# Hand-ordered engine queues, joint key products, token-major second phase and preloaded accumulation banks in a one-core diffusion layer

## The chip, the core and the metric

The kernel runs on one core of a Trainium2 chip. The metric is the device time of one execution in microseconds (us); the median of the runs shown is 2377.83 us. The engines are named as the profile names them: PE is TensorE, PEld its weight load, DVE VectorE, ACT ScalarE, POOL GpSimd, SP the engine whose queue issues the large loads.

## What is computed

One layer of a hybrid backbone over 256 latent tokens and 256 context tokens of width 4096, in float32:

```
mod  = silu(c) @ w_ada + b_ada           # shift, scale, gate: 3 x 4096, for latent and for context
h    = rmsnorm(x) * (1 + scale) + shift  # both streams
z    = h @ w_in                          # 13312 columns
A    = pointwise(silu(layernorm(depthwise31(val * sigmoid(glu)))))
B    = two RG-LRU scans (context first, its last state starts the latent scan)
C    = softmax(q k^T * s + bias) v       # 8x16 window of the latents and all 256 context keys
out  = rmsnorm(x + gate * (concat(A, B, C each * silu(gate path)) @ w_out))
```

From the context only the inputs of the scans (1024 columns), the keys and the values (2048 columns each) are needed. `w_ada` (4096 x 12288) is read once and multiplied by two vectors.

## The kernel before

Every large product takes its float32 operands as two float32r parts, high and low, and makes three passes (high times high, high times low, low times high), `gemm_cm` (L343) and `gemm_tm` (L360). The contraction of 4096 is cut into 32 tiles of 128. Weights come in loads of up to 4 tiles (1 MB, three buffers); ACT copies two tiles to the high part (L338), DVE subtracts to get the low part (L339).

- **Phase 1** goes over ten blocks of the contraction (`BLOCKS`), because the modulation of a tile must be known before its `h` can be made. In each block it makes ten chunks of 512 output columns: `r` (scan inputs, both streams, channel-major, 256-column products for each stream), `k` (keys, context alone, channel-major, 256 columns) and `v` (values, both streams, token-major, 512 columns). At the end of a chunk in a block its PSUM banks are added to SBUF pages by DVE (`spill`, L499; the first block's copies are ACT's, L497). Five banks, tag `g`, serve the chunks in turn.
- **Modulation** (`ada_units`) runs beside it: one load, then one unit of PE work. The two vectors are the stationary operand, padded to 32 columns; the moving operand is up to 512 columns of `w_ada`. Product `k` goes to column group `k % 4` of the array (L217), so that four products of a unit stand on the four groups. The tail of a unit sequence is a copy (L170), transposes (L175) and a sum. The second block of each pair after the eighth has its shift summed on DVE instead.
- **Phase 2** makes latent keys, queries, gates, conv inputs over the whole contraction, all channel-major with 256-column products, and between them the scans, the attention heads (L593 to L617), the depthwise convolution on DVE (L673) and its layer norm.
- **Phase 3** is the output projection, token-major with 512 columns, and the final norm.

The order on each engine is made by the tile framework's scheduler from the order of the code and from `high_priority` sections; `background` (L52) lets the loads of the modulation in at a set rate, `aside` (L490) puts a scan or a convolution between two chunks.

Of the kernel before, what the change touches and what calls it, by code (L numbers as in the profile page):

```python
# [10 lines left out]
F32 = mybir.dt.float32  # L11
# [17 lines left out]
PAIRED = 8  # L29
# [5 lines left out]
HP = 200000  # L35
# rates of the loads that go beside the products, by phase
ADA_A, ADA_B, CAP = 2.15, 1.2, 4.0
G1, G2, G3 = 0.4, 0.3, 0.4
# chunks of the last block that a recurrence follows; order of the second phase
REC1 = (1, 2, 4, 6, 8)  # L40
ORDER = "c0 c1 a0 a1 a2 n a3".split()
# [3 lines left out]
def tile_hybrid_layer(ctx: ExitStack, tc: tile.TileContext, x, c, cctx_tok, c_ctx, w_ada, b_ada,  # L45
# [9 lines left out]
    off = [0]  # L55
    hp = lambda: tc.high_priority(offset=off[0])
    bg = {"q": [], "rate": lambda w: 0.0, "credit": 0.0}

    def background(weight):
        """emits queued units of loads between those of the products, at the set rate"""  # L60
        bg["credit"] = min(bg["credit"] + bg["rate"](weight), CAP)
        while bg["q"] and bg["credit"] >= 2.0:
            bg["credit"] -= 2.0
            bg["q"].pop(0)()
# [5 lines left out]
    def bank(tag, name):  # L70
        uid[0] += 1
        return pp.tile([P, 512], F32, name=f"{name}_{uid[0]}", tag=tag, bufs=5 if tag == "g" else 3)

    def small(n, name):
        uid[0] += 1
        return sp.tile([P, n], F32, name=f"{name}_{uid[0]}", tag="small", bufs=8)

    wada = w_ada[0].rearrange("(k p) n -> p k n", p=P)
# [3 lines left out]
    V, A, S, G = nc.vector, nc.scalar, nc.sync, nc.gpsimd  # L82

    ident = cp.tile([P, P], F32, name="ident")
    make_identity(nc, ident)
    cols = cp.tile([P, 5, P], F32, name="cols")
    where = {}
    q128 = lambda v: v.rearrange("(r q) -> r q", q=P)
    cw_rows = conv_w[0].rearrange("k (t q) -> (k t) q", q=P)
    groups = [  # L90
        [("c", q128(c[0])), ("c_ctx", q128(c_ctx)), ("norm_g", q128(norm_g[0]))],
        [("b_ada", q128(b_ada[0])), ("ln_g", q128(ln_g[0])), ("b_pw", q128(b_pw[0])),
         ("rcb", rconv_b[0].rearrange("d (t q) -> (d t) q", q=P))],
        [("cw0", cw_rows[0:128])],
        [("cw1", cw_rows[128:248]), ("conv_b", q128(conv_b[0]))],
        [("ln_b", q128(ln_b[0])), ("rcw", rconv_w[0].rearrange("d j (t q) -> (d j t) q", q=P)),
         ("lam", lam[0].rearrange("d (t q) -> (d t) q", q=P)),
         ("b_i", b_i[0].rearrange("d (t q) -> (d t) q", q=P)),
         ("b_r", b_r[0].rearrange("d (t q) -> (d t) q", q=P))],
    ]  # L100

    def load_group(gi):
        t = page([P, P], name="rows")
        r = 0
        for name, ap in groups[gi]:
            n = ap.shape[0]
            A.dma_start(t[r:r + n], ap)
            where[name] = (gi, r)
            r += n
        ps = bank("aux", "psc")  # L110
        nc.tensor.transpose(ps[:, :r], t[:r], ident[:r, :r])
        V.tensor_copy(cols[:, gi, :r], ps[:, :r])

    def col(name, i, n=1):
        gi, r = where[name]
        return cols[:, gi, r + i:r + i + n]

    load_group(0)
    load_group(1)
    warm = cp.tile([P, 1], F32, name="warm")  # L120
    A.activation(warm, ident[:, 0:1], AF.Exp)

    # silu(c), silu(c_ctx) as channel columns, padded to 32 stationary columns
    scol = cp.tile([P, 64], F32, name="scol")
    cc64 = cols[:, 0, 0:64]
    V.tensor_scalar(scol, cc64, -80.0, None, ALU.max)
    A.activation(scol, scol, AF.Exp, scale=-1.0)
    V.tensor_scalar(scol, scol, 1.0, None, ALU.add)
    V.reciprocal(scol, scol)
    V.tensor_mul(scol, scol, cc64)  # L130
    cpad = [page([P, 16, 32], name="cpad") for _ in range(2)]
    for i in range(2):
        G.memset(cpad[i], 0.0)
        for s in range(2):
            V.tensor_copy(cpad[i][:, :, s:s + 1],
                          scol[:, 32 * s + 16 * i:32 * s + 16 * i + 16].rearrange("p (k o) -> p k o", o=1))
    sel = cp.tile([P, 2], F32, name="sel")
    for s in range(2):
        V.reduce_sum(sel[:, s:s + 1], ident[:, s:P:32], axis=AX.X)
    mask = cp.tile([P, 2, 64], F32, name="mask")  # L140
    A.dma_start(mask, masks)
    ones = cp.tile([P, 1], F32, name="ones")
    G.memset(ones, 1.0)
    tiny = cp.tile([P, 1], F32, name="tiny")
    G.memset(tiny, 1e-30)
    modG = cp.tile([P, KT, 2], F32, name="modG")
    modS = cp.tile([P, KT, 2], F32, name="modS")
    gcol = cp.tile([P, KT], F32, name="gcol")
    adas = [page([P, 512], name="adas") for _ in range(2)]
    junk = page([P, 512], name="junk")  # L150
    for t in adas + [junk]:
        G.memset(t, 0.0)
    gacc = [cp.tile([P, 512], F32, name=f"gacc{i}") for i in range(2)]

    def accumulate(k, w, n, which):
        """gacc[b] += silu(vector b)[k] * w on the vector engine"""
        for b in which:
            a, s = gacc[b][:, :n], scol[:, 32 * b + k:32 * b + k + 1]
            if k == 0:
                V.tensor_scalar(a, w, s, None, ALU.mult)  # L160
            else:
                V.scalar_tensor_tensor(a, w, s, a, ALU.mult, ALU.add)

# [1 line left out]
    def ada_units(k0, s, parts=(0, 1), on_vector=False):  # L165
        def fin_(part, st):
            srcs = gacc
            if st is not None:
                srcs = [adas[part]]
                V.tensor_copy(adas[part][:, :s * P], st["ps"][:, :s * P])  # L170
            sums = small(8, "sums").rearrange("p (k o) -> p k o", o=2)
            for b, src in enumerate(srcs):
                pm = bank("aux", "psm")
                for i in range(s):
                    nc.tensor.transpose(pm[:, i * P:(i + 1) * P], src[:, i * P:(i + 1) * P], ident)  # L175
                if st is None:
                    V.reduce_sum(sums[:, :s, b:b + 1], pm[:, :s * P].rearrange("p (k n) -> p k n", n=P), axis=AX.X)
                else:
                    V.reduce_sum(sums[:, :s], pm[:, :s * P].rearrange("p (k q o) -> p k o q", q=4, o=32)[:, :, 0:2],
                                 axis=AX.X)  # L180
# [7 lines left out]
        units = []  # L188
        for part in parts:
            c0 = (D if part == 0 else 0) + k0 * P  # L190
            st = {}
            if on_vector:
                def unit(kg, c0=c0):
                    raw = wp.tile([P, 4, 512], F32, name="raw", tag="raw", bufs=NRAW)
                    S.dma_start(raw[:, :, :s * P], wada[:, kg:kg + 4, c0:c0 + s * P])
                    with hp():
                        for j in range(4):
                            accumulate(kg + j, raw[:, j, :s * P], s * P, (0, 1))

                def fin(part=part):  # L200
                    with hp():
                        fin_(part, None)
                units += [lambda kg=kg, u=unit: u(kg) for kg in range(0, KT, 4)] + [fin]
                continue
            W = s * P
            kk = 16 // s // 4 * 4

            def unit(kg, W=W, kk=kk, c0=c0, st=st):
                if "ps" not in st:
                    st["ps"] = bank("aux", "psa")  # L210
# [10 lines left out]
            def fin(part=part, st=st):  # L221
                with hp():
                    fin_(part, st)
# [629 lines left out]
```

## Time and profile before

| what | value |
|---|---|
| three runs, device time | 2375.24, 2377.83, 2378.67 us (median 2377.83) |
| the profiled execution | span 2371.5 us from the first to the last instruction; the median lies 6.3 us above that span |
| PE busy | 2315.1 us, 98% |
| DVE, ACT, POOL busy | 1580.3 us (67%), 945.7 us (40%), 95.8 us (4%) |
| loads | 551.27 MB, 232 GB/s over the span |
| phases by the trace | start 0 to 48.6 us, phase 1 to 935.7, phase 2 to 2003.6, phase 3 to 2371.5 |

A busy PE is not yet a PE at its peak: a matmul's record is longer than the distance to the next one, since matmuls overlap. What a matmul costs is read from the distance between two starts.

### The profile page before, as it was taken

How to read it: one execution, taken by the hardware profiler on the slowest of the kernel's cores; microseconds unless marked ns; L12 is line 12 of the kernel's file. 1: busy time of each engine (PE TensorE's matmuls, PEld its weight loads, DVE VectorE, ACT ScalarE, POOL GpSimd, SP SyncE). 2: the span in 40 equal slices, each digit the busy share in tenths (PEclk: the TensorE clock that was granted, in tenths of full speed). 3: DMA queues.
4: the chain of work that ended last, by engine and by line, in shares of the span. 5: the costliest groups of instructions: out<-in, count | busy, mean ns of one | idle time of the engine just before them, and what ended most of it. 6: DMA issues, size and time to landing. Idle time of an engine off the chain costs nothing.

```text
span 2371.5 us, 38433 instructions
## 1 busy us (share of the span) xinstructions
PE 2315.1 (98%) x16013; PEld 2034.4 (86%) x16013; DVE 1580.3 (67%) x2289; ACT 945.7 (40%) x1228; POOL 95.8 (4%) x150
## 2 busy tenths in 40 slices
PE   6899999999999999999999999999999999999997
PEld 4667777777788998999999899999999999888886
DVE  4465545445778779987879596955766666665555
ACT  5322212222223246886433343344444434434444
POOL 0000000000000001000000101101001001000000
PEclk9999999999999999999999999999999999999999
DMA  9888788877877544656776767767576678775664
GB/s 312 270 279 272 254 298 298 295 266 252 295 269 258 192 163 174 222 183 213 245 233 203 188 215 202 204 215 188 182 245 171 207 265 301 264 263 187 191 192 173
DMA packets 293461, 551.27 MB, mean 232 GB/s; under 512 B 10959, under 2 KB 52647, under 8 KB 293287
## 3 DMA queue, kind: packets, MB, share of 16 engines
q1 hardware_dynamic: 287856, 536.91, 66.1%
q0 software_dynamic: 4480, 11.54, 4.3%
q8 instruction: 125, 2.05, 0.3%
q10 hardware_dynamic: 951, 0.37, 0.1%
q14 instruction: 49, 0.40, 0.0%
HBM read 544.58 MB, written 4.19 MB: 231 GB/s over the span
## 4 chain that ended last, share of the span: by engine, by line
PE 83%; DMA 8%; DVE 4%; ACT 3%; issue 1%; SPq 0%; DVEq 0%; ACTq 0%
PE gcm L355 48%; PE gtm L371 9%; PE gtm L372 8%; PE gtm L370 8%; PE psa L217 5%; DMA raw<-in_w_ada_dram 4%; DMA raw<-in_w_in_dram 3%; DVE lo L339 2%; PE y L614 1%; ACT hi L338 1%; DMA xp<-in_ctx_dram 1%; DVE gacc L245 1%; PE pt L607 1%; PE sc L593 0%; PE sc L594 0%
## 5 line engine op out<-in xcount | busy, mean ns | idle before, releaser
L339 DVE TENSOR_TENSOR lo<-raw,hi 128x1024 fp32r<-128x1024 f32 (+1 forms) x630 | 747.4, 1189 | 556.8 <-ACT hi L338 552.9
L338 ACT CAST hi<-raw 128x1024 fp32r<-128x1024 f32 (+1 forms) x630 | 640.1, 1022 | 1171.9 <-PE gcm L355 492.8
L355 PE MATMUL gcm<-lh,hi 128*128 128x256 f32 x5632 | 1069.5, 285 | 2.9 <-ACT hi L338 2.8
L355 PEld LDWEIGHTS gcm<-lh,hi 128*128 128x128 f32 x5632 | 896.8, 192 | 18.3 <-issue 13.4
L355 PE MATMUL gcm<-lh,lo 128*128 128x256 f32 x2816 | 796.2, 285 | 4.2 <-DVE lo L339 4.0
L355 PEld LDWEIGHTS gcm<-lh,lo 128*128 128x128 f32 x2816 | 537.8, 192 | 11.6 <-DVE lo L339 5.8
L355 PE MATMUL gcm<-ch,hi 128*128 128x256 f32 x1536 | 326.6, 287 | 3.4 <-ACT hi L338 2.3
L355 PEld LDWEIGHTS gcm<-ch,hi 128*128 128x128 f32 x1536 | 259.0, 191 | 36.3 <-issue 27.8
L245 DVE SCALAR_TENSOR_TENSOR gacc<-raw,scol,gacc 128x512 f32<-128x512 f32 x248 | 185.8, 749 | 49.6 <-DMA raw<-in_w_ada_dram 47.1
L355 PE MATMUL gcm<-ch,lo 128*128 128x256 f32 x768 | 217.6, 286 | 0.0
L371 PE MATMUL gtm<-lo,mix 128*128 128x512 f32 x488 | 192.0, 393 | 0.1
L372 PE MATMUL gtm<-hi,mix 128*128 128x512 f32 x488 | 190.1, 390 | 0.0
L370 PE MATMUL gtm<-hi,mix 128*128 128x512 f32 x488 | 171.1, 390 | 0.0
L355 PEld LDWEIGHTS gcm<-ch,lo 128*128 128x128 f32 x768 | 146.5, 191 | 12.8 <-issue 9.0
L217 PE MATMUL psa<-raw,cpad 128*32 128x512 f32 (+3 forms) x1216 | 132.5, 521 | 7.9 <-DMA raw<-in_w_ada_dram 7.8
L499 DVE TENSOR_TENSOR acc<-acc,gcm 128x512 f32<-128x512 f32 x144 | 96.1, 682 | 37.7 <-PE gcm L355 37.1
L371 PEld LDWEIGHTS gtm<-lo,mix 128*128 128x128 f32 x488 | 91.6, 188 | 20.5 <-DVE lo L339 1.3
L370 PEld LDWEIGHTS gtm<-hi,mix 128*128 128x128 f32 x488 | 91.5, 188 | 19.2
L499 DVE TENSOR_TENSOR acc<-acc,gtm 128x512 f32<-128x512 f32 x144 | 94.3, 680 | 19.9 <-PE gtm L372 19.7
L372 PEld LDWEIGHTS gtm<-hi,mix 128*128 128x128 f32 x488 | 91.7, 188 | 18.4
L673 DVE SCALAR_TENSOR_TENSOR cv<-upad,cols,cv 128x256 f32<-128x256 f32 x240 | 105.6, 483 | 0.0
L371 PE MATMUL gtm<-lo,ch 128*128 128x512 f32 x256 | 102.2, 399 | 0.2 <-DVE lo L339 0.2
(218 smaller groups left out, 2107.9 us busy)
## 6 DMA issues: line engine op xcount, KB each, us to landing
raw<-in_w_in_dram SPq DMA_DIRECT2D x210, 1024.0 KB, 5.2
raw<-in_w_ada_dram SPq DMA_DIRECT2D x156, 1024.0 KB, 5.5
raw<-in_w_out_dram SPq DMA_DIRECT2D x61, 1024.0 KB, 5.5
raw<-in_w_ada_dram SPq DMA_DIRECT2D x48, 768.0 KB, 5.9
raw<-in_w_in_dram SPq DMA_DIRECT2D x30, 768.0 KB, 6.1
raw<-in_w_in_dram SPq DMA_DIRECT2D x10, 512.0 KB, 5.4
xp<-in_ctx_dram SPq DMA_DIRECT2D x16, 256.0 KB, 5.8
xp<-in_x_dram SPq DMA_DIRECT2D x16, 256.0 KB, 5.4
```

Source lines behind the costliest of these rows:

```text
L217: nc.tensor.matmul(st["ps"][32 * q:32 * q + 32, :W], cpad[k // 16][:, k % 16, :], raw[:, j, :], start=(k < 4), stop=(k >= KT - 4))
L245: V.scalar_tensor_tensor(st["a"], raw[:, j], s, st["a"], ALU.mult, ALU.add)
L338: A.copy(hi[:, :n], raw[:, o:o + n])
L339: V.tensor_sub(lo[:, :n], raw[:, o:o + n], hi[:, :n].bitcast(F32))
L355: nc.tensor.matmul(banks[r // 2][:, (r % 2) * T:(r % 2) * T + T], w[:, j, nt * P:(nt + 1) * P], movs[m][k][:, part], start=first, stop=las ...
L370: nc.tensor.matmul(banks[b], hh, wh[:, j], start=first, stop=False)
L371: nc.tensor.matmul(banks[b], hh, wl[:, j], start=False, stop=False)
L372: nc.tensor.matmul(banks[b], hl, wh[:, j], start=False, stop=last)
L499: V.tensor_add(acc[key, i], acc[key, i], b)
L607: nc.tensor.transpose(ps[:, kt * T + qt * P:kt * T + qt * P + P], Ps[qt][:, (2 * kp + kt) * P:(2 * kp + kt + 1) * P], ident)
L614: nc.tensor.matmul(ps[:, :T], acc[("v", h // 4), kt][:, i * P:(i + 1) * P], Ps[kt // 2][:, (kt % 2) * T:(kt % 2) * T + T], start=(kt == 0) ...
L673: V.scalar_tensor_tensor(o, upad[n][:, tap:tap + T], cw(tap, n), o, ALU.mult, ALU.add)
```

## The change

The engine queues are written out by hand (`manual_schedule`): a step is up to two tiles of the contraction of one chunk; side work runs in generators ("threads") that are advanced between products as long as two counters, one for DVE and one for ACT, say that the engine has time. Further:

- latent keys move from phase 2 to phase 1, so that `r` and `k` both take 512-column products over both streams (`both`); the latent values move from phase 1 to phase 2;
- phase 2 is token-major with 512-column products; what is needed channel-major is turned back by PE transposes (`turned`);
- a chunk of a later block preloads most of its banks with the sums so far (ACT writes PSUM), and ACT copies them back at its end; one bank a chunk is still added by DVE;
- phase 1 has 13 blocks; loads have 512 KB, in six buffers; a modulation unit has two products where it is 384 or 512 columns wide, four at 256, eight at 128; DVE sums the shift of the last sixteen tiles;
- the gate part of the modulation is summed over 1024 columns in one instruction.

```diff
-BLOCKS = [1, 2, 3, 3, 3, 4, 4, 4, 4, 4]
-NPG, NRAW, NHI = 75, 3, 3
+BLOCKS = [1, 1, 2, 2, 3, 3, 3, 3, 3, 3, 3, 3, 2]
+MODS = [(1, 1, 0), (2, 2, 0), (4, 2, 0), (6, 3, 0), (9, 3, 0), (12, 4, 0), (16, 4, 1), (20, 4, 1), (24, 4, 1),
+        (28, 4, 1)]
+NPG, NWD, NRAW, NHI = 69, 6, 6, 3
...
-            kk = 16 // s // 4 * 4
...
+        def mod_matmuls(ps, raw, k, n, W):
+            for j in range(n):
+                q = (k + j) % 4
+                mm(ps[32 * q:32 * q + 32, :W], cpad[(k + j) // 16][:, (k + j) % 16, :], raw[:, j, :],
...
+                self.n = 2 if s > 2 else 8 // s
...
+                if ch.kind == "both":
+                    sl = slice(b * P, (b + 1) * P)
+                    one(o, wh[:, j, sl], H4[k][:, 0], st, False)
+                    one(o, wh[:, j, sl], H4[k][:, 1], False, False)
+                    one(o, wl[:, j, sl], H4[k][:, 0], False, sp_)
...
+        def spill(ch, key):
+            for i, b in enumerate(ch.banks):
+                if i in ch.pre:
+                    A.copy(acc[key, i], b)
+                elif (key, i) not in acc:
+                    acc[key, i] = page([P, 512], name="acc")
+                    (A.copy if i % 2 else V.tensor_copy)(acc[key, i], b)
+                else:
+                    V.tensor_add(acc[key, i], acc[key, i], b)
...
+        def preload(ch, key):
+            for i in sorted(ch.pre):
+                ch.banks[i] = bank("g" + ch.kind, "g")
+                A.copy(ch.banks[i], acc[key, i])
...
+                    ch.pre = {1} if kind == "v" else {1, 2, 3}
...
+        def turned(tm, i):
+            ps = bank("turn")
+            for j in range(2):
+                for b in range(2):
+                    tr(ps[:, j * T + b * P:j * T + b * P + P], tm[b][:, (i + j) * P:(i + j + 1) * P], ident)
```

How the order of instructions moves, at three places. On PE before, around a modulation unit in a block of phase 1 (`gtm` are banks of a `v` chunk, `psa` the modulation's sums):

```order
L371 MATMUL gtm_414_4683<-lo_4730,ch_356_3762 128x512
L372 MATMUL gtm_414_4683<-hi_4729,ch_356_3762 128x512
L370 MATMUL gtm_414_4683<-hi_4729,ch_359_3771 128x512
L371 MATMUL gtm_414_4683<-lo_4730,ch_359_3771 128x512
L217 MATMUL psa_401_4636<-raw_4825,cpad_6_100 32x512 x4
L372 MATMUL gtm_414_4683<-hi_4729,ch_359_3771 128x512
L370 MATMUL gtm_415_4684<-hi_4729,ch_356_3762 128x512
```

Before, the units are 72 runs of four at 512 columns, 48 of four at 384, 8 of eight at 256. On PE after, at the end of a `v` chunk and the head of the `k` chunk behind it, with such a unit (`gboth` are banks of a chunk over both streams):

```order
L421 MATMUL gtm_967_4656<-hi_962_4618,h4_870_4149 128x512
L421 MATMUL gtm_967_4656<-lo_965_4633,h4_870_4149 128x512
L421 MATMUL gtm_967_4656<-hi_962_4618,h4_870_4149 128x512
L421 MATMUL gboth_983_4709<-h4_868_4139,hi_970_4662 128x512 x2
L421 MATMUL gboth_983_4709<-h4_868_4139,lo_972_4673 128x512
L266 MATMUL psa_883_4194<-raw_953_4573,cpad_4_90 32x512 x2
L421 MATMUL gboth_983_4709<-h4_869_4144,hi_970_4662 128x512 x2
L421 MATMUL gboth_983_4709<-h4_869_4144,lo_972_4673 128x512
L421 MATMUL gboth_976_4695<-h4_868_4139,hi_970_4662 128x512 x2
```

After, a unit holds two products: 96 runs of two at 512 columns, 64 of two at 384, 32 of four at 256, 8 of eight at 128 behind the start. The new bank `gboth_983` is given the place in PSUM of `gtm_967`, whose last product is the row just ahead of it. On ACT after, at the same place:

```order
L858 COPY gtm_967_4656<-acc_145_707 128x512
L406 CAST hi_970_4662<-raw_943_4502 128x1024
L406 CAST hi_974_4683<-raw_947_4539 128x512
L848 COPY acc_145_707<-gtm_967_4656 128x512
L858 COPY gboth_976_4695<-acc_156_753 128x512
L858 COPY gboth_977_4697<-acc_157_755 128x512
L858 COPY gboth_978_4699<-acc_158_757 128x512
```

The copy out of `gtm_967` (L848) comes ahead of the three preloads of the next chunk (L858); PE's first product into `gboth_983` waits for that copy.

## Rows read from the trace of the kernel before

**Rows 1.** The page's head and its first part, busy time by engine.

```profile
span 2371.5 us, 38433 instructions
PE 2315.1 (98%) x16013; PEld 2034.4 (86%) x16013; DVE 1580.3 (67%) x2289; ACT 945.7 (40%) x1228; POOL 95.8 (4%) x150
```

**Rows 2.** Busy time in four stretches: length, each engine, granted clock, DMA share, GB/s.

```profile
0.00:48.60 48.60, 27.09 (x281) 20.99 (x281) 26.75 (x64) 27.77 (x73) 3.09 (x13) 0.96 0.99 310
48.60:935.70 887.10, 877.15 (x5761) 688.48 (x5762) 547.08 (x847) 246.00 (x320) 8.72 (x16) 1.00 0.75 259
935.70:2003.60 1067.90, 1055.62 (x8390) 1032.65 (x8389) 792.26 (x1133) 518.96 (x652) 81.26 (x116) 1.00 0.68 214
2003.60:2371.50 367.90, 355.20 (x1586) 292.29 (x1584) 214.17 (x248) 152.98 (x184) 2.67 (x5) 0.99 0.65 213
```

**Rows 3.** PE's waits by releaser: total us, times, longest.

```profile
PE psa L217 <- DMA raw<-in_w_ada_dram: 7.8, 8, 2.5
PE gcm L355 <- ACT hi L338: 5.1, 3, 2.8
PE y L614 <- ACT pr L611: 4.3, 1, 4.3
PE pt L607 <- DVE pr L601: 0.9, 1, 0.9
```

**Rows 4.** Groups of instructions by line and shape: the 256-column products.

```profile
L355 PE MATMUL gcm<-lh,hi 128*128 128x256 f32 x5632 | 1069.5, 285 | 2.9 <-ACT hi L338 2.8
L355 PE MATMUL gcm<-lh,lo 128*128 128x256 f32 x2816 | 796.2, 285 | 4.2 <-DVE lo L339 4.0
L355 PE MATMUL gcm<-ch,hi 128*128 128x256 f32 x1536 | 326.6, 287 | 3.4 <-ACT hi L338 2.3
L355 PE MATMUL gcm<-ch,lo 128*128 128x256 f32 x768 | 217.6, 286 | 0.0
```

**Rows 5.** Timeline of PE in phase 2, 256 columns: start, length, what.

```profile
1996.29 0.28 PE L355 MATMUL gcm<-lh,lo 128*128 128x256 f32 x1
1996.41 0.40 PE L355 MATMUL gcm<-lh,hi 128*128 128x256 f32 x2
1996.65 0.28 PE L355 MATMUL gcm<-lh,lo 128*128 128x256 f32 x1
```

**Rows 6.** Timeline in phase 1, end of a `v` chunk, 512 columns.

```profile
840.62 0.39 PE L371 MATMUL gtm<-lo,lh 128*128 128x512 f32 x1
840.84 0.39 PE L372 MATMUL gtm<-hi,lh 128*128 128x512 f32 x1
841.07 0.28 PE L355 MATMUL gcm<-ch,hi 128*128 128x256 f32 x1
841.27 1.05 ACT L338 CAST hi<-raw 128x1024 fp32r<-128x1024 f32 x1 [4.38 <-PE gtm L372]
```

**Rows 7.** Timeline of PE, a modulation unit of four products, 512 columns.

```profile
423.13 0.28 PE L355 MATMUL gcm<-lh,hi 128*128 128x256 f32 x1
423.34 1.07 PE L217 MATMUL psa<-raw,cpad 128*32 128x512 f32 x8
424.33 0.38 PE L355 MATMUL gcm<-ch,lo 128*128 128x256 f32 x1
424.56 0.28 PE L355 MATMUL gcm<-lh,lo 128*128 128x256 f32 x1
```

**Rows 8.** The same at 384 columns.

```profile
133.30 0.28 PE L355 MATMUL gcm<-ch,hi 128*128 128x256 f32 x1
133.50 0.85 PE L217 MATMUL psa<-raw,cpad 128*32 128x384 f32 x8
134.51 0.28 PE L355 MATMUL gcm<-ch,lo 128*128 128x256 f32 x1
```

**Rows 9.** Timeline of PE, single float32 products of 512 columns (a scan's gates).

```profile
1097.15 1.02 PE L444 MATMUL pr<-rec,gw 128*128 128x512 f32 x2
1098.01 1.02 PE L446 MATMUL pi<-rec,gw 128*128 128x512 f32 x2
```

**Rows 10.** Timeline: PE released by ACT; and the copy of a bank, by line.

```profile
60.69 0.62 ACT L338 CAST hi<-raw 128x512 fp32r<-128x512 f32 x1 [2.34 <-DMA raw<-in_w_in_dram]
61.36 0.50 PE L370 MATMUL gtm<-hi,ch 128*128 128x512 f32 x1 [0.65 <-ACT hi L338]
L497 ACT COPY acc<-gcm 128x512 f32<-128x512 f32 x16 | 8.6, 591 | 3.2 <-PE gcm L355 3.1
```

**Rows 11.** Timeline of PE, transposes of 128 columns.

```profile
738.67 0.27 PE L175 MATMUL psm<-ident,adas 128*128 128x128 f32 x1
738.78 0.27 PE L175 MATMUL psm<-ident,gacc 128*128 128x128 f32 x1
```

More of the change, by code (lines that the diff above doesn't have):

```diff
@@ L102, in load_group @@
[L102 to L162, printed above, removed]
@@ L165, in ada_units @@
[L165 to L180, printed above, removed]
+    mm, tr = nc.tensor.matmul, nc.tensor.transpose
@@ new lines, in run_threads, with drain @@
+    def run_threads():
+        for th in list(threads):
+            if th.at <= clock["tick"]:
+                advance(th, th.rank == 0)
+    def drain(*ths):
+        for _ in range(2000):
+            if all(t.done for t in ths):
+                return
+            for t in list(threads):
+                if not t.done and (t in ths or t.rank == 0 or clock["aux"] > 0):
+                    advance(t, True)
+            clock["tick"] += 1
+        raise RuntimeError("a thread waits for ever")
@@ new lines, in mod_finish_vector @@
+        def mod_finish_vector(k0, s):
+            sums = small(8, "sums").rearrange("p (k o) -> p k o", o=2)
+            for b in range(2):
+                yield from take(1)
+                pm = bank("psm")
+                for i in range(s):
+                    tr(pm[:, i * P:(i + 1) * P], gboth[:, b, i * P:(i + 1) * P], ident)
+                yield None
+                V.reduce_sum(sums[:, :s, b:b + 1], pm[:, :s * P].rearrange("p (k n) -> p k n", n=P), axis=AX.X)
+                give(1)
+                yield 0.7, 0
+            mod_columns(1, k0, s, sums)
+            yield 0.2, 0
@@ new lines, in tile_hybrid_layer, with conv_in @@
+        places, cvp = [], []
+        def conv_in(g, vals, glu):
+            for b in range(2):
+                V.scalar_tensor_tensor(vals[0][b], glu[0][b], 1.0, vals[0][b], ALU.add, ALU.mult)
+                yield 0.7, 0
+            unpair(glu)
+            yield None
+            if not places:
+                for _ in range(2):
+                    w = wide([P, 4, T], name="conv")
+                    places.extend(w[:, i] for i in range(4))
+                    cvp.extend(w[:, i:i + 2] for i in (0, 2))
+                wides[0] += 2
+                places.append(page([P, T], name="conv"))
+            for i in (0, 2):
+                yield from take(1)
+                ps = turned(vals[0], i)
+                yield None
+                for j in range(2):
+                    A.copy(places[4 * g + i + j + 1], ps[:, j * T:(j + 1) * T])
+                give(1)
+                yield 0, 0.8
+            unpair(vals)
@@ new lines, in gate_rec @@
+        def gate_rec(g, sil, before):
+            while not all(t.done for t in before):
+                yield None
+            yield None
+            for i in (0, 2):
+                yield from take(1)
+                ps = turned(sil[0], i)
+                yield None
+                n = 4 * g + i
+                yb = acc[("r", g), i]
+                V.scalar_tensor_tensor(yb, yb, 0.5, ps, ALU.mult, ALU.mult)
+                give(1)
+                yield 0.75, 0
+                yield None
+                split_mix([8 + n, 8 + n + 1], yb)
+                yield 0.9, 0.8
+            unpair(sil)
@@ new lines, in tile_hybrid_layer, with __init__, items, start @@
+        end1 = t
+        class Mod:
+            def __init__(self, part, k0, s, vec):
+                self.part, self.k0, self.s, self.vec = part, k0, s, vec
+                self.thread = None
+                bi = max(i for i in range(len(BLOCKS)) if starts[i] <= k0)
+                self.due = begin[bi] - (0.5 * (begin[bi] - begin[bi - 1]))
+                self.n = 2 if s > 2 else 8 // s
+            def items(self):
+                return [ModItem(self, k) for k in range(0, KT, self.n)]
+            def start(self):
+                if not self.vec:
+                    self.ps = bank("psa")
```

1495 lines of the change are left out of this document (929 added, 566 removed).

## The prediction

> **What bounds the kernel now.** I read the page's first part, then the stretches, then PE's waits, then single places of the timeline. The first part shows PE busy for 2315.1 of 2371.5 us, DVE for 67% and ACT for 40% [rows 1]. The stretches show the same in each phase: PE is busy for 877 of 887 us in phase 1 and for 1056 of 1068 us in phase 2, while DVE has 547 and 792 us of work and ACT 246 and 519 us [rows 2]. The reader should look at PE's waits next: behind the start its longest entries add up to some 18 us, and none of them names the sum of a bank into its page (L499) [rows 3]. So PE is the limit, nearly gapless, and the change is judged by two questions: does it take PE work away, and does it make PE wait?
>
> A busy PE says little about the price of a product, so prices come from distances between starts. Three products of 256 columns start 0.36 us apart from the next three, 0.120 us each [rows 5]. Products of 512 columns start 0.22 to 0.23 us apart (840.62, 840.84, 841.07); I take 0.227 us, 0.013 less than two halves [rows 6].
>
> **The change part by part.** The sum is made against the profiled span of 2371.5 us; the median of the runs lies 6.3 us above it, and I carry that over at the end.
>
> *Full-width products.* The groups of 256-column products over the two streams count 5632 + 2816 + 1536 + 768 = 10752 [rows 4]. All of them become half as many of 512 columns: keys of both streams in one moving operand, phase 2 token-major. 10752 x 0.120 = 1290.2 us become 5376 x 0.227 = 1220.4 us: **-69.9 us**, all on the path. The moved keys and values change phase, not number. The pointwise product and the output projection keep their shapes.
>
> *Modulation units.* A unit of four products at 512 columns lies between starts at 423.13 and 424.56; take away the two ordinary products there (0.24) and it costs 1.19 us [rows 7]. The same at 384 columns: 134.51 - 133.30 - 0.24 = 0.97 us [rows 8]. The eight records of the first unit are two passes of four products side by side. A single float32 product of 512 columns also needs two passes, and its neighbour starts 0.86 us later [rows 9]: one product alone takes as long as four on the four column groups. So a unit of two should cost what a unit of four costs, 0.86 us and a fixed 0.33 us for going in and out. Before there are 72 x 1.19 + 48 x 0.97 + 8 x 1.19 = 141.8 us; the eight-product units at 256 columns are twice two passes of half length, which is why they get 1.19 as well. After: 96 x 1.19 + 64 x 0.97 + 32 x 0.76 + 8 x 0.76 = 206.7 us, with 0.76 as 0.43 + 0.33 for two passes of 256 columns. That is **+64.9 us**, although DVE takes over more of the shifts. From below the unit of two would cost half of its neighbour of four: 110 us in all, -32 us. I take the equal price, since the nearest row is the single product.
>
> *Transposes.* Turning back takes 112 transposes and the modulation has 12 more; two starts lie 0.11 us apart [rows 11]. 124 x 0.11 = **+13.6 us**.
>
> *Bank swaps.* Here the change adds a wait. In the order after, 33 of the swaps from a `v` chunk to a chunk over both streams, and 6 between two of the latter, give the new chunk's first bank the place of the bank that PE has just finished; PE's next product waits for ACT's copy out of it, and everything behind it on PE waits too. Price: after the last product of 512 columns started (840.84), ACT starts its next work at 841.27, 0.43 us later [rows 6]; the copy of a bank takes 0.59 us, and PE starts 0.05 us after an ACT instruction that it waited for (60.69 + 0.62 to 61.36) [rows 10]. 0.43 + 0.59 + 0.05 - 0.227 = 0.84 us, 39 times: 33 us. Nine more wait for a bank that ended three products earlier (0.16 us each), and the second bank of a `v` chunk waits behind three copies and a preload on ACT against six products of PE, some 0.07 us in 48 cases: 5 us. Together **+38 us**. The lower bound is 39 x 0.59 = 23 us; the upper, with one cast of 1.05 us ahead of each copy on ACT, 79 us. I take the bare chain, because ACT has room: 246 us in phase 1 and 264 preloads, 264 copies back at 0.59 us make about 540 us in more than 900.
>
> What this buys is nothing on the path: some 170 DVE adds fewer, while DVE has a third of its time free and PE's waits name none of them [rows 2, 3]. The Trainium skill ("TensorEngine Tiling (Array Packing)", Performance Considerations, on the PSUM bottleneck) advises to let both ScalarE and VectorE empty PSUM; by that rule the swaps should get shorter and cost nothing, which is the second rival below. The trace of before speaks against a gain, since no wait for emptying stands there to be shortened.
>
> *Hand-overs of the side threads in phase 2.* Sixteen heads give PE four joints each (two scores, transposes, values), the scans 16, the turning 28: 108 places where PE, in order, takes the result of ACT or DVE that was issued a product or two earlier. The trace has two such waits, 0.9 and 4.3 us [rows 3]. The bounds are 0 and 108 x 0.9 = 97 us; I take 0.2 us each, **+22 us**, since the counters keep both engines from falling far behind.
>
> *Start.* The first loads of tokens are issued ahead of those of `w_ada`; but the first 48.6 us run at a DMA share of 0.99 [rows 2], and the bytes needed are the same. The tokens (2 x 256 x 4096 x 4 bytes) and the first tile's part of `w_ada` (4096 x 256 x 4) are 12.6 MB; at 310 GB/s they would take 41 us, so up to 8 us could be won; I take **-4 us**. DMA later on is covered: phase 1 used 0.75 of the DMA, and the same bytes in a longer phase need no more. Six buffers of 512 KB hold what three of 1 MB held. DVE's other moves (more shifts, fewer adds) leave it near 60% of phase 1, beside PE; without that cover a late low part would show as a PE wait for `lo`. The wider gate sums and the new place of the last square sums lie off PE: nothing.
>
> The sum: -69.9 + 64.9 + 13.6 + 38 + 22 - 4 = +64.6, a span of 2436 us; with 6.3 us around it **2442 us**.
>
> **The rivals.**
>
> *Units priced by their columns (faster).* If a unit of two costs half a unit of four, the modulation falls by 32 instead of rising by 65. The place is every `psa` unit of phase 1. The time is 2442 - 97 = **2345 us**. For it: the four products of a unit do overlap, so the array shares something. Against: the single product takes the full 0.86 us [rows 9]. It decides the sign as soon as a unit of two at 512 columns costs less than about 0.8 us.
>
> *PE stays full (no change).* Bank swaps and hand-overs cost nothing, because PE's queue is fed earlier than the order suggests: 2442 - 60 = **2382 us**. For it: before, PE waits for ACT and DVE for a few microseconds in all. Against: the copy cannot begin before the product ahead of PE's waiting one has ended.
>
> *Side threads come late.* DVE already works 792 of 1068 us in phase 2 [rows 2]; if each joint costs the 0.9 us of the observed wait, +75 us: **2517 us**. For it: a wait of this sort holds all products behind it. Against: the longest sums of such waits before are single events.
>
> That the change does not do what it says is excluded by the order: 2304 products over both streams, 264 preloads and 112 turning transposes stand there.
>
> **How the numbers follow.** I give the forecast 0.63, the faster rival 0.09, the full PE 0.13, the late threads 0.15. About 0.2% (4.8 us) is what a measurement of this kernel can tell from no change. The full PE lies at that edge; I split it 0.03 faster, 0.07 same, 0.03 slower. So faster 0.12, same 0.07, slower 0.81. The bounds of swaps, hand-overs and start around the forecast reach from about 2400 to 2500 us. The range of eight in ten is 2378 to 2520 us: it leaves out the faster rival and a little of the full PE below, and the far end of the late threads above.
>
> **What would show it.** In the profile after: starts of the `gboth` and `gtm` products 0.227 us apart; a `psa` record group of four instead of eight, with still some 1.19 us between its neighbours; PE waits for the copies of L848, near 0.8 us, about forty times; phase 1 near 970 us, phase 2 near 1050, the output projection unchanged near 355. The prediction is wrong if phase 1 is shorter than the 887 us of before, or if units of two cost about 0.6 us, or if PE's list of waits names neither L848 nor the hand-overs.

## The result and the profile after

The changed kernel takes 2495.32 us (median of four runs, 2492.68 to 2498.70), the kernel before 2377.47 us beside it: a ratio of 1.0500, interval 1.0485 to 1.0515. It is slower by 118 us; forecast were 65 us more, 2442 us, in a range up to 2520. The profiled spans are 2490.9 and 2371.5 us, 119.4 us apart.

The head and the first part of the page after, to be held against [rows 1]:

```profile
span 2490.9 us, 29941 instructions
PE 2377.0 (95%) x10761; PEld 1751.9 (70%) x10761; DVE 1596.2 (64%) x2204; ACT 1241.3 (50%) x1830; POOL 93.5 (4%) x133
```

PE has a third fewer instructions and is busy for 62 us longer; its idle time has doubled, from 56 to 114 us. Where this lies is told by the same four stretches as in [rows 2] (start, phases 1 to 3: length, PE, PEld, DVE, ACT, POOL, granted clock, DMA share, GB/s):

```profile
0.00:50.25 50.25, 30.03 (x264) 21.49 (x264) 26.09 (x60) 27.68 (x73) 2.64 (x12) 0.93 0.99 302
50.25:1049.90 999.65, 951.04 (x4185) 598.58 (x4186) 533.27 (x844) 513.81 (x860) 6.54 (x12) 0.99 0.70 217
1049.90:2117.50 1067.60, 1037.12 (x4705) 835.23 (x4704) 800.49 (x1051) 547.12 (x715) 81.08 (x103) 0.99 0.73 215
2117.50:2490.90 373.40, 358.84 (x1610) 296.66 (x1608) 236.31 (x252) 152.65 (x183) 3.24 (x6) 0.99 0.73 238
```

Phase 1 makes nearly all of it: +112.6 us. The start is 1.7 us longer, phase 2 is unchanged (-0.3), phase 3 takes 5.5 us more. PE stands idle for 48.6 us in phase 1, where it was 10 before, and for 30.5 in phase 2, where it was 12. PE's waits after (total us, times, longest), to be held against [rows 3]:

```profile
PE gboth L421 <- ACT acc L848: 32.9, 43, 2.2
PE pt L667 <- ACT pr L658: 16.8, 21, 2.9
PE gtm L421 <- DVE lo L412: 12.2, 11, 2.5
PE psm L292 <- DVE gboth L921: 6.4, 3, 2.9
PE gboth L421 <- DVE acc L853: 3.8, 3, 3.3
```

The first entry is the swap of banks that the prediction spoke of, the second one kind of hand-over in the attention heads. The swap itself, on PE and ACT, at the end of a `v` chunk:

```profile
308.08 0.39 PE L421 MATMUL gtm<-lo,h 128*128 128x512 f32 x1
308.31 0.40 PE L421 MATMUL gtm<-hi,h 128*128 128x512 f32 x1
308.80 0.59 ACT L848 COPY acc<-gtm 128x512 f32<-128x512 f32 x1 [1.79 <-PE gtm L421]
309.44 0.73 PE L421 MATMUL gboth<-h,hi 128*128 128x512 f32 x2 [0.73 <-ACT acc L848]
310.00 0.40 PE L421 MATMUL gboth<-h,lo 128*128 128x512 f32 x1
```

From the last product to the next one are 1.13 us instead of 0.23, so the swap costs 0.90 us (the chain of the prediction gave 0.84). Then the two products behind the wait take 0.56 us (309.44 to 310.00) where two take 0.47 elsewhere (425.23 to 425.70 below): another 0.1 us. ACT had been idle for 1.79 us before the copy, so it was not late. The list of waits names 0.73 of the 0.90 us: it counts from the end of the last record, 0.40 us behind its start, where the next product would otherwise have started after 0.23. So a named wait costs some 0.17 us more than is named, and 0.1 us behind it, 0.27 in all.

The modulation units of 512 columns (records, busy us, mean ns), after and before:

```profile
L266 PE MATMUL psa<-raw,cpad 128*32 128x512 f32 x384 | 101.0, 605 | 0.0
L217 PE MATMUL psa<-raw,cpad 128*32 128x512 f32 x576 | 76.7, 605 | 0.4 <-DMA raw<-in_w_ada_dram 0.4
```

384 records in 96 units of two products (four records) take 101.0 us; before, 576 records in 72 units of four took 76.7 us. And one unit on PE's timeline, with a stretch of ordinary products:

```profile
423.11 0.40 PE L421 MATMUL gboth<-h,lo 128*128 128x512 f32 x1
423.43 1.05 PE L266 MATMUL psa<-raw,cpad 128*32 128x512 f32 x4
424.42 0.74 PE L421 MATMUL gboth<-h,hi 128*128 128x512 f32 x2
425.00 0.40 PE L421 MATMUL gboth<-h,lo 128*128 128x512 f32 x1
425.23 0.63 PE L421 MATMUL gboth<-h,hi 128*128 128x512 f32 x2
425.70 0.39 PE L421 MATMUL gboth<-h,lo 128*128 128x512 f32 x1
```

425.00 to 425.70 are three products, 0.23 us each. 423.11 to 425.00 are three products and the unit: 1.89 - 0.68 = 1.21 us, for two products where [rows 7] has 1.19 us for four.

One more thing differs, for which the prediction has no term: the clock that TensorE is granted. Its mean is 0.994 of full speed in the profile before and 0.988 in the one after. An estimate from these: 0.006 x 2371.5 = 14 us of full-speed time are missing before and 0.012 x 2490.9 = 30 us after, so up to 16 of the 119 us are the clock's; what of it falls into waits costs nothing. One such place in phase 2, behind a long wait for scaled probabilities (PE's timeline, then a stretch of it with the columns of [rows 2]):

```profile
1441.02 0.33 PE L667 MATMUL pt<-ident,pr 128*128 128x128 f32 x1 [2.18 <-ACT pr L658]
1443.06 0.63 PE L421 MATMUL gtm<-lo,lh 128*128 128x512 f32 x1
1443.48 1.05 PE L421 MATMUL gtm<-hi,lh 128*128 128x512 f32 x2
1444.34 0.63 PE L421 MATMUL gtm<-lo,lh 128*128 128x512 f32 x1
```

```profile
1442.30:1445.70 3.40, 3.40 (x11) 2.72 (x10) 2.03 (x3) 0.22 (x1) 0.00 (x0) 0.51 0.54 114
```

The granted clock is 0.51 there, the lower of its two levels (1.2 GHz) but for the edges, and three products take 1.28 us (1443.06 to 1444.34) instead of 0.68, 0.43 us each. Such stretches add up to 27 us of phase 2 after and to 10 us before; 17 us more of them cost some 17 x (1 - 0.227 / 0.43) = 8 us.

### The profile page after: what moved, and what is told of

Same layout as the page of the kernel before. It is cut to its first block, busy times and chain, and to the rows that moved or that the text cites. A ratio compares the mean times of both kernels' runs of the same rounds, so it can differ in the third digit from the quotient of the medians.

```text
span 2490.9 us, 29941 instructions
## 1 busy us (share of the span) xinstructions
PE 2377.0 (95%) x10761; PEld 1751.9 (70%) x10761; DVE 1596.2 (64%) x2204; ACT 1241.3 (50%) x1830; POOL 93.5 (4%) x133
## 4 chain that ended last, share of the span: by engine, by line
PE 62%; DVE 5%; ACT 3%; issue 2%; DMA 2%; POOL 0%; ACTq 0%; DVEq 0%; POOLq 0%
PE gtm L421 45%; PE gboth L421 10%; DVE lo L412 2%; DMA B<-in_rpb_dram 1%; PE psa L266 1%; ACT hi L406 1%; PE gcm L421 1%; PE sc L644 1%; PE y L682 1%; ACT acc L848 1%; PE pr L525 1%; PE pi L527 1%; PE pt L667 0%; DVE gboth L1116 0%; DMA raw<-in_w_in_dram 0%
## 5 line engine op out<-in xcount | busy, mean ns | idle before, releaser
L421 PE MATMUL gtm<-hi,lh 128*128 128x512 f32 x2560 | 839.1, 403 | 0.2
L421 PEld LDWEIGHTS gtm<-hi,lh 128*128 128x128 f32 x2560 | 486.4, 190 | 111.2 <-issue 10.1
L421 PE MATMUL gboth<-h,hi 128*128 128x512 f32 x1536 | 503.8, 409 | 40.3 <-ACT acc L848 32.9
L421 PE MATMUL gtm<-lo,lh 128*128 128x512 f32 x1280 | 505.7, 395 | 12.5 <-DVE lo L412 12.2
L421 PEld LDWEIGHTS gboth<-h,hi 128*128 128x128 f32 x1536 | 273.4, 189 | 209.7 <-issue 93.5
L421 PE MATMUL gboth<-h,lo 128*128 128x512 f32 x768 | 302.6, 394 | 0.0
L421 PEld LDWEIGHTS gtm<-lo,lh 128*128 128x128 f32 x1280 | 243.4, 190 | 78.1 <-DVE lo L412 20.3
L848 ACT COPY acc<-gboth 128x512 f32<-128x512 f32 x216 | 125.7, 587 | 141.4 <-PE gboth L421 130.7
L421 PE MATMUL gtm<-hi,h 128*128 128x512 f32 x512 | 187.4, 410 | 2.5 <-ACT acc L848 1.6
L921 DVE SCALAR_TENSOR_TENSOR gboth<-raw,scol,gboth 128x512 f32<-128x512 f32 x248 | 168.8, 746 | 0.0
L1116 DVE SCALAR_TENSOR_TENSOR gboth<-raw,scol,gboth 128x1024 f32<-128x1024 f32 x124 | 158.5, 1278 | 0.0
L858 ACT COPY gboth<-acc 128x512 f32<-128x512 f32 x216 | 117.5, 594 | 0.0
L421 PEld LDWEIGHTS gtm<-lo,mix 128*128 128x128 f32 x488 | 92.1, 189 | 18.9 <-DVE lo L412 0.2
```

Source lines behind the costliest of these rows:

```text
L421: one = lambda o, l, r, start, stop: mm(o, l, r, start=start, stop=stop, skip_group_check=True)
L848: A.copy(acc[key, i], b)
L858: A.copy(ch.banks[i], acc[key, i])
L921: V.scalar_tensor_tensor(a, self.raw[:, j], s, a, ALU.mult, ALU.add)
L1116: V.scalar_tensor_tensor(a, self.raw, s, a, ALU.mult, ALU.add)
```

## The experiments

All but the last kernel are edits of the changed one (2495.3 us). Each was timed beside the kernel before, which stood at 2375.8, 2375.1 and 2374.3 us in the three sets (2377.5 in the first), so a difference between sets carries 2 to 3 us of that.

### Units of four again

```diff
-                return [ModItem(self, k) for k in range(0, KT, self.n)]
+                step = 4 if self.s > 2 and not self.vec else self.n
+                return [ModItem(self, k) for k in range(0, KT, step)]
...
-                    mod_matmuls(m.ps, self.raw, self.k, m.n, m.s * P)
+                    for i, raw in enumerate(self.raws):
+                        mod_matmuls(m.ps, raw, self.k + i * m.n, m.n, m.s * P)
...
```

> Edit: the changed kernel, but two loads of two products each are issued together and their four products stand next to each other in PE's order, at 384 and 512 columns; loads keep their size, all else stays. Theory (a unit of two costs what a unit of four costs, because its products on two column groups take as long as products on four): 48 units of 1.18 us and 32 of 0.98 us fall away, 88 us, so 2495 - 88 = 2407 us; groups of eight psa records keep near 1.18 us at 512 columns. Rival (the price goes by the products, and only the going in and out, 0.33 us a unit, is saved): 80 x 0.33 = 26 us less, 2469 us, with about 1.9 us for a unit of four. Second rival (two loads in a row hold back the weights): PE waits for loads of w_in or for high parts grow by 20 us or more and take back part of the gain, 2425 to 2450 us.

2428.57 us, ratio 1.0231 (1.0213 to 1.0249): 67 us less. In the groups by shape, the row of the 512 columns:

```profile
L266 PE MATMUL psa<-raw,cpad 128*32 128x512 f32 x384 | 53.2, 614 | 0.0
```

A unit on PE's timeline, between ordinary products:

```profile
427.17 0.39 PE L421 MATMUL gboth<-h,lo 128*128 128x512 f32 x1
427.49 1.06 PE L266 MATMUL psa<-raw,cpad 128*32 128x512 f32 x8
428.48 0.73 PE L421 MATMUL gboth<-h,hi 128*128 128x512 f32 x2
429.05 0.39 PE L421 MATMUL gboth<-h,lo 128*128 128x512 f32 x1
```

PE's waits in phase 1 that grew:

```profile
PE gtm L421 <- DVE acc L853: 9.9, 3, 4.8
PE gboth L421 <- DVE acc L853: 7.6, 8, 2.6
```

The same 384 records need half the time, and a unit of eight records costs 429.05 - 427.17 - 0.68 = 1.20 us. The equal price is shown: 88 us of PE's work fall away. Of these, 21 come back. 13 are waits for DVE's adds (L853: 17.5 us, 4.2 without this edit); DVE's work of phase 1, 532 us, now stands in 934 instead of 1000 us. Some 6 are the clock's by the estimate above (0.985 x 2424.6 against 0.988 x 2490.9 us: 36 against 30 us missing). The second rival's range is the one that was met, but it named the wrong late party: the loads were in time.

### The first bank in another place

First, the first bank merely asked for ahead of the preloaded ones; second, each bank emptied as soon as it is done, with preloads ahead of the chunk's last step:

```diff
-            for i in sorted(ch.pre):
+            for i in range(ch.nb):
                 ch.banks[i] = bank("g" + ch.kind, "g")
-                A.copy(ch.banks[i], acc[key, i])
+                if i in ch.pre:
+                    A.copy(ch.banks[i], acc[key, i])
```

> Edit: the changed kernel, but the first bank of a new chunk is taken ahead of the preloaded ones, so that it gets the place that is already free, and a preloaded bank gets the place of the bank finished last. Theory (PE waits at a swap because of the place its first bank is given): the waits for L848 (32.9 us, 43 times) all but vanish; the first preloaded bank now comes behind one copy out on ACT and is needed 0.7 to 1.4 us after the swap, so new waits for L858 of some 0.3 to 0.5 us stand at about 48 swaps, 15 to 24 us; the time falls by 20 to 30 us, to 2465 to 2475 us. Rival (ACT itself is behind at the swaps, with casts ahead of the copies): the waits only change their name, from L848 to L858, and the time stays within 8 us of 2495.

2495.35 us, no difference, and the first row of PE's waits is the same to the digit (32.9 us, 43 times). This run is void as a test: PE's first product of the new chunk still waits for the copy out of the bank of the `v` chunk's last product, so the first bank still lies there. Asking in another order did not move it.

```diff
...
+                if tail and ch.block is not None and j == n - 1:
+                    ch.after(b)
+                    if before and b:
+                        before()
...
```

> Edit: the changed kernel, but each bank of a chunk in phase 1 is copied out or added as soon as its own last product is issued instead of at the chunk's end, banks of the next chunk are taken in their order, and as many preloads as there are free places are issued ahead of the chunk's last step. Theory (the swaps cost what they cost because copy out and preload stand in a row behind the last product): the first two or three banks of the next chunk are ready when PE comes to them, waits for L848 and L858 fall from 35 us to under 8, and the time falls by 40 to 50 us, to 2445 to 2455 us. Rival (copies and preloads that stand earlier on ACT come ahead of the high parts and make these late): PE waits for hi or lo of 15 us or more appear, 2475 us or above.

2482.80 us, 12.5 us less. Expected were 40 to 50. The time lies in the rival's range, but not for its reason: waits for low parts are 12.1 us, 12.2 without the edit. PE waits 19.2 us for L849 and 17.0 us for L854 (the copy and the add, one line further down), 22 times each: the first bank again got one of the two places of the `v` chunk, now either. So both were run again with the places given out in a fixed turn (the second with its early preloads from the second block on):

```diff
+        if tag == "g":
+            place[0] = (place[0] + 1) % 5
+            tag = f"g{place[0]}"
...
```

> Edit: the changed kernel, but the five banks of a chunk's products are given out in a fixed turn (five names of one bank each), and a chunk takes its first bank ahead of the preloaded ones; so the first bank of a new chunk lies in a place that has long been free, and the preloaded bank that is needed last takes the place of a finished one. Preloads and copies stay where they are on ACT. Theory (the place of the first bank makes PE wait): waits for L848 fall from 32.9 us to under 5; the first preloaded bank stands behind one copy out on ACT and is needed 0.7 to 1.4 us after the swap, so some 48 waits of 0.3 to 0.5 us appear for L858 instead; 2465 to 2475 us. Rival (it is ACT's row of copies, whatever the place): waits keep their sum under another name, and the time stays within 8 us of 2495.

> Edit: as in the run with the fixed turn of the five banks, and in addition each bank is copied out or added as soon as its own last product is issued, and the preloads that find a free place are issued ahead of the chunk's last step. Theory (place and order on ACT together make the swaps): both parts mended, PE's waits for L848, L853 and L858 together fall below 10 us from 41, and the time comes within 8 us of the kernel without preloads, 2434 to 2445 us. Rival (copies among the casts of ACT make high parts late): waits for hi or lo of 15 us or more, 2460 us or above.

2461.55 us (1.0359, 1.0331 to 1.0388) and 2446.30 us (1.0302, 1.0286 to 1.0317): 34 and 49 us less. PE's longest waits in phase 1 of the first, and of the second:

```profile
PE gtm L426 <- ACT gtm L864: 13.7, 9, 3.1
PE psm L297 <- DVE gboth L927: 9.5, 3, 5.7
PE gboth L426 <- ACT gboth L864: 4.1, 3, 2.7
```

```profile
PE gtm L426 <- ACT gtm L866: 7.2, 7, 2.2
PE psm L297 <- DVE gboth L929: 6.5, 3, 3.0
```

No wait for a copy out is left. What stays are waits for preloads: in the first kernel 12 instead of the 48 expected, but longer, 17.8 us in all (L864), in the second 8.2 us (L866). The second stays 12 us above the kernel without preloads (next section), where at most 8 were expected. The pairs with and without the fixed turn differ by 33.8 and 36.5 us; the place of the first bank is therefore the larger part of what the swaps cost. Copying and preloading earlier gives another 12.5 to 15 us.

### No preloads

```diff
-                    ch.pre = {1} if kind == "v" else {1, 2, 3}
+                    ch.quota = 1 if kind == "v" else 3
...
```

(`quota` stands for `len(ch.pre)` in the counters alone.)

> Edit: the changed kernel without preloaded banks in phase 1: every bank of a chunk is added to its page by DVE, none is copied in or out by ACT; the counters that pace the side threads are left as they were. Theory (preloading buys nothing on the path and costs the swaps): PE's waits for L848 and L858 vanish (35 us by name, 45 to 50 us with the slow products around them), DVE gets 264 more adds of about 0.68 us in phase 1 (528 to some 708 of 1000 us) and still keeps up; 2445 to 2460 us. Rival (DVE would be late with the adds and with the low parts, which is what the preloads are there for): PE waits for L853 and for lo reach 40 us or more, 2490 us or above.

2434.56 us, ratio 1.0256 (1.0241 to 1.0272): 61 us less, more than the 35 to 50 expected. By the profiles 56 of them lie in phase 1, and start and phase 3 give back 4. Another 6 lie in phase 2, which the edit leaves alone: the stretches at the lower clock add up to 14 us there, not 27, which makes some 6 us. Phase 1 and PE's waits in it:

```profile
51.10:994.30 943.20, 930.58 (x4185) 603.51 (x4186) 691.49 (x1108) 236.41 (x333) 6.51 (x12) 0.99 0.71 230
```

```profile
PE psm L292 <- DVE gboth L921: 5.9, 2, 4.1
PE psm L278 <- DVE adas L271: 4.0, 2, 3.6
PE gtm L421 <- DVE acc L853: 2.7, 3, 1.1
```

DVE takes 158 us more, ACT 277 us less, and PE waits 2.7 us for the adds. The same swap now, `v` chunk to `gboth`, without a gap (302.80 to 303.03):

```profile
302.80 0.40 PE L421 MATMUL gtm<-hi,h 128*128 128x512 f32 x1
303.03 0.62 PE L421 MATMUL gboth<-h,hi 128*128 128x512 f32 x2
303.49 0.40 PE L421 MATMUL gboth<-h,lo 128*128 128x512 f32 x1
```

Against the changed kernel, PE's idle time in phase 1 falls by 36 us and its busy time by 20 us, at the same 4185 instructions. The 44 waits for copies out explain 12 of these 20, at the 0.27 us that each costs beyond its name. The clock is not the reason, 0.99 in both; the other 8 stay open.

### Both together

> Edit: units of four products and no preloads together. Theory (the two costs are separate; each is PE's own time): the differences of the two single runs add up, 2495 - 67 - 61 = 2367 us, 0.4% below the kernel before. Rival (DVE sets a second limit in a shorter phase 1: its 528 us of work and 180 us of adds stand against some 870 us, and the run with units of four already showed PE waiting 17 us for L853 where it had waited 4): waits for DVE, by adas, gboth, acc or lo, add up to 40 us or more in phase 1, and the time is 2385 us or above.

2370.74 us, ratio 0.9982 (0.9971 to 0.9993): the differences of the single runs add up, within 4 us. In phase 1 (878.5 us, DVE busy for 687.6) PE's waits for DVE add up to 23.5 us (L853 9.4, the modulation's sums 12.4, low parts 1.7), where the rival asked for 40.

### A later hand-over in the attention heads

```diff
                     sums.append(sm)
-                yield None
                 for qt in range(2):
                     V.reciprocal(sums[qt], sums[qt])
                     A.mul(Ps[0][qt], Ps[0][qt], sums[qt])
                     yield 0.1, 0.6
                 yield None
+                yield None
                 yield from take(2)
```

> Edit: the changed kernel, but in each attention head the step that hands the scaled probabilities from ACT to PE's transposes waits one piece of products longer (three products of 512 columns, 0.68 us), and the step between the exponentials and the scaling one piece less. Theory (PE reaches the transposes before ACT has scaled the probabilities, because ACT's queue is about one instruction behind there): the waits for L658 (16.8 us, 21 times) fall by half to two thirds, 2482 to 2488 us. Rival (ACT is several instructions behind, with casts of 1 us ahead): the sum of these waits stays within 4 us, and the time within 4 us of 2495.

2474.83 us, ratio 1.0420 (1.0400 to 1.0439): 20 us less, where 7 to 13 were expected. One such joint in the changed kernel (ACT scales two tiles, PE transposes them):

```profile
1469.22 0.39 PE L421 MATMUL gtm<-hi,lh 128*128 128x512 f32 x1
1469.45 1.33 ACT L658 ACTIVATE pr<-pr,sm 128x512 f32<-128x512 f32 x2 [1.43 <-DVE sm L657]
1470.23 0.33 PE L667 MATMUL pt<-ident,pr 128*128 128x128 f32 x1 [0.62 <-ACT pr L658]
1470.84 0.98 PE L667 MATMUL pt<-ident,pr 128*128 128x128 f32 x7 [0.28 <-ACT pr L658]
1471.58 0.48 PE L421 MATMUL gtm<-hi,lh 128*128 128x512 f32 x1
```

2.36 us from product to product; the product and eight transposes need 0.23 + 0.88, so 1.25 us are lost, while the list of waits names 0.90 of them. ACT starts in the moment it is asked and needs 1.33 us for its two tiles: it is not behind at this joint, PE comes too early. With the later step phase 2 is 18.9 us shorter, and its waits for the scaled probabilities (L657 now) are:

```profile
PE pt L667 <- ACT pr L657: 6.0, 11, 2.1
```

That is 10.8 us and ten waits less by name, some 3 us more at 0.27 each. The other 5 go with the clock: the stretches at its lower level add up to 14 instead of 27 us of phase 2, worth 6 us, and the one shown above is gone.

### The versions put together

> Edit: units of four, no preloads, and the later transposes of the attention heads together. Theory (three separate costs of PE's own time): 2371 - 20 = 2351 us, 1.0% below the kernel before. Rival (a shorter phase 1 and a DVE that carries all adds push work into phase 2, where ACT and DVE are then further behind at the heads): waits for L658 or L657 stay above 12 us, 2362 us or above.

> Edit: units of four, the preloads kept with the fixed turn of the banks and the early copies, and the later transposes. If the preloads relieve DVE where it sets a limit in the shorter phase, this kernel is the faster of the two: fewer waits for L853 and for the modulation's sums on DVE than without preloads, 2340 to 2350 us. If DVE sets no limit, the differences of the single runs add up, 2495 - 67 - 49 - 20 = 2359 us, slower than its counterpart without preloads (2351 us) by the 11 us by which the two single runs differ.

2353.71 us, ratio 0.9915 (0.9902 to 0.9927), without preloads; 2363.14 us, ratio 0.9954 (0.9942 to 0.9967), with them, in the fixed turn. They lie 6 and 4 us above the sums of the single differences. Relieving DVE does not pay even in the shorter phase: its adds make PE wait 8.2 us in the first kernel (L853) and not at all in the second, which waits 9.6 us for preloads (L866) and 5.2 for late high parts instead. Preloading is the slower way there too. The first lies 20.6 us below the kernel before and is the version to take from this study; the next one is shorter, but changes part of the computation.

> Edit: units of four, no preloads, later transposes, and in addition the transposes of the modulation's sums wait two pieces of products longer (five for the sums that DVE makes). Theory (PE waits there for a DVE that is one or two instructions behind, 14.5 us for adas and gboth in the run with units of four and no preloads): these waits fall below 5 us, and the time is 8 to 10 us below its counterpart, 2341 to 2343 us. Rival (the sums are needed at once for the next block's h, so that the wait only moves to the head of the block): the waits for adas and gboth fall, but waits for h come in their place, and the time stays within 4 us.

2345.62 us, ratio 0.9877 (0.9861 to 0.9892), 8.1 us below its counterpart. In this kernel the sum that DVE makes of the shifts of tiles 24 to 27 is begun anew for the next four tiles before it has been turned, so these four shifts are not the reference's; the work is the same, and the time can be compared. The waits for the sums fall from 14.9 us (L278 and L292) to:

```profile
PE psm L281 <- DVE adas L271: 3.7, 4, 1.7
PE psm L297 <- DVE gboth L930: 1.0, 1, 1.0
```

Waits for low parts ahead of `gboth` products grow by 4.4 us (2.0 to 6.4), and the clock's mean is 0.991 where it was 0.988, so a part of the 8 us may be the clock's. The waits for late sums look like a cost of the same kind as those in the heads; a version that uses it needs a second buffer for DVE's sums, which wasn't tried.

### The kernel before with units of two

```diff
-            kk = 16 // s // 4 * 4
+            kk = 2 if s > 2 else 16 // s // 4 * 4
```

> Edit: the kernel before, with two products in a unit and a load instead of four where it is 384 or 512 columns wide (loads of 384 and 512 KB into the three buffers of 1 MB); nothing else. Theory (a unit of two costs what a unit of four costs): 72 more units of 1.19 us and 48 of 0.97 us, 132 us more, 2507 us, if all of these units lie beside products as before. Rival (the price goes by the products): 120 x 0.33 = 40 us more, 2415 us. Loads of half the size in the same three buffers may be late as well: then PE's waits for raw, 7.8 us before, grow by 15 us or more, and the time lies above 2520 us.

2573.25 us, ratio 1.0847 (1.0830 to 1.0863): 199 us more. The groups of 512 columns, and the longest wait:

```profile
L217 PE MATMUL psa<-raw,cpad 128*32 128x512 f32 x576 | 157.8, 637 | 22.9 <-DMA raw<-in_w_ada_dram 22.9
```

```profile
PE psa L217 <- DMA raw<-in_w_ada_dram: 50.6, 43, 2.6
```

576 records took 76.7 us in units of four and take 157.8 in units of two: the price doubles in this kernel as well, worth 132 us by the units. Beyond it, loads of half the size in the same three buffers come late, 43 us more by name, as the third case said. The remaining 24 us fit the clock: its mean is 0.980, so 51 us of full-speed time are missing where it was 14, though part of that falls into the waits.

## Why the prediction was right, and where it was off

**What bounds the kernel** held: PE stays the limit, and what an edit took from PE's work or waits left the time, but for the 21 us under the units of four. The range held and the sign was right, but the change of 118 us is nearly twice the 65 that were forecast: several terms were too small, and one, the clock, was missing.

**Full-width products** (-69.9): the price came as worked out, 0.227 us in phase 2 (three in 0.68 us, 1699.78 to 1700.46) and 0.23 in the places shown from phase 1. That the whole term came is not shown, since no run takes these products back alone, nor the 13 blocks.

**Modulation units** (+64.9) came as worked out, 1.21 against 1.19 us a unit. In the forecast this term decided the sign. In the kernel it does not do so alone: units of four give 67 us back and leave it 2.3% slower. The rival by columns is excluded by two kernels. The Trainium skill ("TensorE: Matmul & The Clock Gate", Part 3 on packing small matmuls) gives for a pack one product's duration and some 4 ns for each further tile; by that a unit of four would cost some 0.02 us more than one of two, an estimate for its two passes. The runs agree that the two cost about the same (1.20 and 1.21 us).

**Bank swaps** (+38) is the term that was mis-sized most: taking the preloads out gives 61 us, 56 of them in phase 1, inside the bounds of 23 and 79. The chain was right (0.90 us measured for 0.84); the slow restart behind each wait was missing, and so were swaps into banks that DVE adds (4.2 us, L853). That preloading buys nothing on the path was right: DVE makes all the adds and its other work in 691 of 943 us. The Trainium skill advises to let both engines empty PSUM ("TensorEngine Tiling (Array Packing)", Performance Considerations). In this case DVE alone is faster, 2434.6 against 2495.3 us, and still by 12 us with the places mended; but ACT copies each sum in again besides, so a mere sharing of the emptying, without preloads, is not tested here.

**Hand-overs in phase 2** (+22): without this term the prediction's numbers put phase 2 at 1030 us (7680 of the 10752 products lie there, -49.9 us, and 112 transposes, +12.3); it took 1067.6, so some 37 us are left for this term and for all that has none. PE's waits named in phase 2 rise from 12 us (10 times) to 30 (34 times), which makes 18 us and some 6 at 0.27 each; the lower clock makes 8. The few others weren't traced. Spread evenly over 108 joints the term was wrong in kind: moving the 16 joints of the scaled probabilities alone gives 18.9 us back, and the waits for low parts grew from 4 [rows 4] to 12 us.

**Start** (-4): the first product stands at 50.3 instead of 48.6 us, with loads at 302 instead of 310 GB/s; no gain from asking for tokens first is to be seen. **DVE beside PE** ("nothing"): DVE's sums of shifts make PE wait 6.4 us (L292), a wait of the kind that the prediction named as its sign for `lo` only. **Phase 3** (unchanged) is 5.5 us longer: half of the gate's column sums (L1127) fall there now, a quarter before, 1.9 us more with 1.9 us of waits; the rest weren't traced.

Of the 55 us that were missing, phase 1 has 28 (forecast near 970, it took 1000 us), phase 2 has 15, start and phase 3 have 6 each. In phase 1, 18 are the swaps (56 for 38) and some 6 the late sums. The rival in which PE stays full is excluded by the first two rows of PE's waits; that of the late threads asked for 97 us of hand-overs, far above the 37 found.

## What to carry to other kernels

Price a packed group of small products by its passes, not by its products, before halving a load. When a bound engine works in order, look at where the allocator puts the next result, not only at who empties it; relieving an engine that keeps up gained nothing here. When a bound engine waits, look at its clock behind the wait too. A step that hands over to such an engine should come one piece of its work later than the helper needs.

## What was not expected of the hardware

A product behind a wait of PE is followed 0.1 us later than usual (0.56 for 0.46 us over two products). Taking waits out gives back more than the list of waits names: 20 us for 10.8 in the heads, 61 for about 40 at the swaps. Part of it is the 0.27 us that each wait costs beyond its name, part the granted clock, which was at its lower level behind the wait of 2.18 us in the head shown. Not of the hardware: asking for banks in another order did not change their places, which made two kernels test something else than they were written for.
